# A three-layer kernel on one core: more yield points in the RWKV chain, a scan and two exponentials in halves, later transposes in stick-breaking attention

## The chip, the cores and the metric

The kernel runs on one core of a Trainium2 chip. The metric is the device time of one execution in microseconds (us), as the median of three runs. A core has TensorE (PE in the rows below), VectorE (DVE), ScalarE (ACT), GpSimd (POOL) and SyncE (SP), each with its own instruction stream that is worked off in order; they wait for each other through semaphores.

## What is computed

Three layers follow each other on 1024 tokens of width 1024, all in float32: a block with three mixing branches (stick-breaking attention, and two gated linear recurrences), a block with an RWKV-7 time mix and a dilated window attention, and a block with spatial gating and a Fourier mix. Two parts bear on the change. Stick-breaking attention, per head and per block of 128 queries:

```python
log_one_minus = jnp.where(causal, jax.nn.log_sigmoid(-z), 0.0)
tail = lax.cumsum(log_one_minus, axis=3, reverse=True) - log_one_minus
weights = masked_exp(causal, log_beta + tail)
outs.append(jnp.einsum('bhts,bhsd->bhtd', weights, vb.astype(jnp.float32)))
```

and the RWKV time mix, a recurrence over tokens for 16 heads of 64, followed by a group norm:

```python
def step(state, inp):
    r_t, w_t, k_t, v_t, av_t, bv_t = inp
    sa = jnp.einsum('bhvk,bhk->bhv', state, av_t)
    state = (state * w_t[:, :, None, :] + sa[..., None] * bv_t[:, :, None, :]
             + v_t[..., None] * k_t[:, :, None, :])
    return state, jnp.einsum('bhvk,bhk->bhv', state, r_t)
mu = jnp.mean(y, axis=-1, keepdims=True)
var = jnp.mean(jnp.square(y - mu), axis=-1, keepdims=True)
y = ((y - mu) * lax.rsqrt(var + GN_EPS)).reshape(B, S, RWKV_W) * ln_x_w + ln_x_b
```

## The kernel before, in words

**Dense products.** Large projections are split into a high and a low part and formed by three matmuls (L304 to L306). `dense_gen` makes such a product for 128 output columns and all tokens; it yields after every three matmuls. These rows are the bulk of TensorE's work and depend on little else; here they are called dense rows.

**How work is interleaved.** Each piece of work is a Python generator. `interleave` takes a list of generators, each with a number of steps and a range, and always advances the one whose position `a + (b - a) * steps done / steps given` is lowest. The order in which instructions are written is a priority: when the program is built, a scheduler puts the instructions of every engine into a fixed order, by that priority and by its own estimate of when operands are ready. A generator with more steps than it was given ends up behind the others, which are then exhausted.

**Stick-breaking (`stick`, twice, 8 query blocks each).** For a query block and two heads: score matmuls (L548), two sigmoids per score tile on ACT (L549, L550), on DVE a mask, a product scan over up to 1024 columns (L557) and a multiplication (L558); then 128x128 transposes on TensorE (L569), copies of these out of PSUM on DVE (L571), and the products with the values (L577). The generator is given 60 steps and has 60.

**RWKV (`rwkv`).** There are 16 units (8 head pairs by 2 halves of the tokens), in 18 iterations. In iteration `it` stand, interleaved: `rw_chain` of unit `it - 2`, `rw_inverse` of unit `it - 1`, `rw_feat` of unit `it`, and dense rows. Iterations 14 and 15 have fewer dense rows than the earlier ones, because the projections of head pair 8 do not exist.

`rw_chain` is a recurrence over 8 hops. One hop is: two products with the state (L1149) into PSUM; a copy of one half by DVE (L1150, tile R) and of the other by ACT (L1151, the scheduler lets it wait for DVE's); the product L1154; again a copy by DVE (L1155, tile SV) and by ACT (L1156); the products L1158 and L1163; and two DVE operations (L1162) that make the next state, on which the next hop's L1149 waits. There is one yield after each hop. Behind the last hop come the group norm (DVE, ACT, one power on POOL at L712), `GNY` = 4 yields, transposes (L1184) and a gate. The chain is given 11 + `GNY` = 15 steps.

`rw_feat` makes, among others, the decay: two products (L977, L978), two tanh on ACT, a scaling on POOL (L983), a scan of 512 columns on DVE (L985, a running sum within chunks of 64), two exponentials on ACT (L989, L990).

Of the kernel before, what the change touches and what calls it, by code (L numbers as in the profile page):

```python
# [12 lines left out]
AF = mybir.ActivationFunctionType  # L13
ALU = mybir.AluOpType
# [158 lines left out]
L3 = (0.2, 1.1)  # L173
WB = [(4,), (5, 3), (4,), (5,), (5,), (4, 3)]
MRB = 2
GNY = 4
V3 = (0.0, 0.8)
YD = 0
LNP = 4
# [15 lines left out]
PLAN = [(0.0, 1.0), (0.0, 0.5), (0.05, 0.8), (0.0, 1.0)]  # L195


class Kern:
# [328 lines left out]
    def stick(self, pm, pr, q, k, v, y):  # L527

        nc = self.nc
        for i in range(NT):  # L530
            W = 128 * (i + 1)
            bes = []
            qs = self.t(pm, [128, 2, 2, 128], "q2", F32R, bufs=1)
            for h in range(2):
                r = slice(64 * h, 64 * h + 64)
                src = q[r, 128 * i:128 * i + 128]
                for d in (r, slice(64 - 64 * h, 128 - 64 * h)):
                    nc.scalar.copy(qs[d, h, 0], src)
                for d in (slice(0, 64), slice(64, 128)):
                    nc.vector.tensor_tensor(qs[d, h, 1], src, qs[r, h, 0].bitcast(F32), ALU.subtract)  # L540
            for h in range(2):
                be = self.t(pm, [128, T], "be", bufs=3)
                om = self.t(pm, [128, T + 1], "om", bufs=2)
                for s0 in range(0, W, 512):
                    n = min(512, W - s0)
                    z = self.mm_ps()[:, :n]
                    for m in range(2):
                        nc.tensor.matmul(z, qs[:, h, m], k[h][:, s0:s0 + n], start=m == 0, stop=m == 1)  # L548
                    nc.scalar.activation(be[:, s0:s0 + n], z, AF.Sigmoid, scale=0.125)  # L549
                    nc.scalar.activation(om[:, s0:s0 + n], z, AF.Sigmoid, scale=-0.125)  # L550
                    yield
                dg = slice(W - 128, W)
                nc.vector.tensor_tensor(om[:, dg], om[:, dg], self.c("mge"), ALU.max)
                nc.vector.tensor_tensor(be[:, dg], be[:, dg], self.c("mlt"), ALU.mult)
                nc.gpsimd.memset(om[:, W:W + 1], 1.0)
                omr = om[:, W - 1::-1]
                nc.vector.tensor_tensor_scan(omr, omr, omr, 1.0, ALU.mult, ALU.min)  # L557
                nc.vector.tensor_tensor(be[:, :W], be[:, :W], om[:, 1:W + 1], ALU.mult)  # L558
                bes.append(be)
                yield  # L560
            po = self.mm_ps()[:, :128]
            for g0 in range(0, i + 1, 4):
                ws = []
                for b0 in range(g0, min(g0 + 4, i + 1), 2):
                    bl = [(h, b) for b in range(b0, min(b0 + 2, i + 1)) for h in range(2)]
                    wt = self.t(pm, [128, 4, 128], "wt", bufs=3)
                    pt = self.mm_ps()
                    for n, (h, b) in enumerate(bl):
                        nc.tensor.transpose(pt[:, 128 * n:128 * n + 128], bes[h][:, 128 * b:128 * b + 128], self.ident)  # L569
                    nb = len(bl)  # L570
                    nc.vector.tensor_copy(wt[:, :nb].rearrange("p a b -> p (a b)"), pt[:, :128 * nb])  # L571
                    ws.append((bl, wt))
                    yield
                for bl, wt in ws:
                    for n, (h, b) in enumerate(bl):
                        r = slice(64 * h, 64 * h + 64)
                        nc.tensor.matmul(po[r, :], v[:, b, 128 * pr + 64 * h:128 * pr + 64 * h + 64], wt[:, n], start=b == 0, stop=b == i)  # L577
            sl = slice(128 * i, 128 * i + 128)
            nc.vector.tensor_tensor(y[:, sl], po, y[:, sl], ALU.mult)
# [334 lines left out]
    def rwkv(self):  # L914
        nc, tc, I = self.nc, self.tc, self.I
        with tc.tile_pool(name="rw", bufs=1, reuse_waits="tile") as rw, self.psum(mx=2, iv=1, ch=1, cy=1):
            if RO:
                for n, shape, b in RORD:
                    self.t(rw, shape, n, bufs=b)
            self.consts(rw, "c2")  # L920
            self.XS = [self.t(rw, [128, 8, 128], f"XS{n}") for n in range(2)]
            self.SV = [self.t(rw, [128, 8, 2, 64], f"SV{n}") for n in range(2)]
            for x in self.XS:
                nc.gpsimd.memset(x, 0.0)
            for a in self.first:
                self.dense_fm(*a, hfs=(1,))
            for h in range(2):
                nc.scalar.activation(self.lov[h][0:64], self.lov[h][0:64], AF.Tanh)
            U = [dict(p=u // 2, hf=u % 2, u=u) for u in range(16)]
            self.jp = rw  # L930
            att = iter(self.att_jobs())
            for it in range(18):
                gens = []
                if it >= 2:
                    gens.append((self.rw_chain(rw, U[it - 2]), 11 + GNY, *PLAN[0]))
                if 1 <= it <= 16:
                    gens.append((self.rw_inverse(rw, U[it - 1]), 37, *PLAN[1]))
                if it < 16:
                    gens.append((self.rw_feat(rw, U[it]), 20, *PLAN[2]))
                jobs = list(islice(att, ATT[it]))  # L940
                gens.append((chain(*jobs, self.rw_dense(rw, it)), 32 * (it < 16) + 16 * len(jobs), *PLAN[3]))
                interleave(gens)
            self.late_jobs = list(att)
        self.rk_pool.__exit__(None, None, None)
# [18 lines left out]
    def rw_feat(self, rw, S):  # L963
        nc, I = self.nc, self.I
        V, TT = nc.vector, nc.vector.tensor_tensor
# [4 lines left out]
        c8 = lambda a: a.rearrange("p (c t) -> p c t", c=8)  # L970
        E, O = slice(0, 64), slice(64, 128)
        cc = float(np.exp(-0.5))
# [7 lines left out]
        sg, ta = ff("fs"), ff("ta")  # L980
# [1 line left out]
        nc.scalar.activation(ta, aps, AF.Tanh, bias=self.ha0[:, p:p + 1], scale=0.5)  # L982
        nc.gpsimd.tensor_scalar(sg, sg, 0.5, 0.5, ALU.mult, ALU.add)  # L983
        yield
        V.tensor_tensor_scan(sg, self.c("cm"), sg, 0.0, ALU.mult, ALU.add)  # L985
        e1 = self.t(rw, [128, 8, 65], "E1")
        ei = ff("ei")
        nc.gpsimd.memset(e1[:, :, 0:1], 1.0)
        nc.scalar.activation(e1[:, :, 1:65], c8(sg), AF.Exp, scale=-cc)  # L989
        nc.scalar.activation(ei, sg, AF.Exp, scale=cc)  # L990
        S["dc"] = dc = self.t(rw, [128, 8], "dc", bufs=3)
        nc.gpsimd.tensor_copy(dc, e1[:, :, 64])
        yield
# [46 lines left out]
        for c0 in (0, 4):  # L1040
            cs = slice(c0, c0 + 4)
# [84 lines left out]
    def rw_chain(self, rw, S):  # L1126
        nc = self.nc
        V, TT = nc.vector, nc.vector.tensor_tensor
# [7 lines left out]
        c8 = lambda a: a.rearrange("p (c t) -> p c t", c=8)  # L1136
# [6 lines left out]
        for c in range(8):  # L1143
            up, sp = [self.mm_ps("ch")[:, 0:w] for w in (64, 128)]
            sd = self.t(rw, [128, 64], "sd", bufs=2)
            R = self.t(rw, [128, 64], "R", bufs=2)
            dc = dcs[:, c:c + 1]
            for n, s in enumerate((E, O)):
                nc.tensor.matmul(xy[:, c, n], M1[:, c, n], sv[:, c, n], start=c % 4 == 0 and n == 0, stop=False, skip_group_check=True)  # L1149
            V.tensor_copy(R[E], xy[E, c, 0])  # L1150
            nc.scalar.copy(R[O], xy[O, c, 1])  # L1151
            for n, s in enumerate((E, O)):
                nc.scalar.activation(sd[s], sv[s, c, n], AF.Identity, scale=dc[s])  # L1153
            nc.tensor.matmul(up, xs[:, c], R, start=True, stop=True)  # L1154
            V.tensor_copy(sv[E, c, 0], up[E])  # L1155
            nc.scalar.copy(sv[O, c, 1], up[O])  # L1156
            both = sv[:, c].rearrange("p n v -> p (n v)")
            nc.tensor.matmul(sp, M3[:, c].rearrange("p n k -> p (n k)"), both, start=True, stop=True)  # L1158
            for n, s in enumerate((E, O)):
                if not (hf == 1 and c == 7):  # L1160
                    so = sv[s, c + 1, n] if c < 7 else svn[s, 0, n]
                    V.scalar_tensor_tensor(so, sp[s, 64 * n:64 * n + 64], dc[s], sd[s], ALU.mult, ALU.add)  # L1162
            nc.tensor.matmul(xy[:, c].rearrange("p n v -> p (n v)"), A[:, c], both, start=False, stop=c % 4 == 3, skip_group_check=True)  # L1163
            yield
# [6 lines left out]
        V.tensor_scalar(st[:, 0:8], st[:, 0:8], -1.0 / 64, None, ALU.mult)  # L1171
        TT(c8(y), c8(y), bc(st[:, 0:8]), ALU.add)
        nc.scalar.activation(sq, y, AF.Square)
        yield
        V.tensor_reduce(st[:, 8:16], c8(sq), AX.X, ALU.add)
        self.rsqrt(rw, st[:, 16:24], st[:, 8:16], 1.0 / 64, 64e-5)
        TT(c8(y), c8(y), bc(st[:, 16:24]), ALU.mult)
        for _ in range(GNY):
            yield
# [520 lines left out]
```

## Time and profile before

| | us |
|---|---|
| median of 3 runs | 2867.9 (2866.1 to 2868.88) |
| the profiled execution | 2864.67 |
| its span, first to last instruction | 2862.9 |
| PE busy | 2753.2 (96%) |
| DVE busy | 1754.1 (61%) |
| ACT busy | 1168.3 (41%) |
| POOL busy | 278.4 (10%) |

The profile shows one execution. Busy time of PE is a sum of modelled durations: a dense row is shown 0.39 us long while the next starts 0.23 us later, so a busy PE is not a PE at its peak. The stick-breaking part lies between about 60 and 330 us of the span, the RWKV part between about 920 and 2000 us; the chains run from 1070 us on.

### The profile page before, as it was taken

The page shows a single profiled execution, that of the slowest core. Times are in us where ns is not written, and L with a number is a line of the kernel's source. Part 1 is how long each engine was busy: PE and PEld are TensorE (multiplying, and loading weights), DVE is VectorE, ACT ScalarE, POOL GpSimd, SP SyncE. Part 2 cuts the span into 40 slices and gives each one's busy share as a digit, 9 for nine tenths or more (in the row PEclk, how much of TensorE's full clock was granted, in tenths as well). Part 3 has the DMA queues.
Part 4 walks back from the last instruction along what each step waited for, and adds up shares of the span by engine and source line. Part 5 has one row for each costly group of instructions (what it writes and reads, how often), then busy time and mean ns, then how long its engine had stood idle before and what let it go on. Part 6 is the DMA issues. An engine that isn't in the chain of part 4 may idle for free. (4 is left out here: it accounts for less than half of the span.)

```text
span 2862.9 us, 51271 instructions
## 1 busy us (share of the span) xinstructions
PE 2753.2 (96%) x19572; PEld 2303.7 (80%) x19572; DVE 1754.1 (61%) x4639; ACT 1168.3 (41%) x2830; POOL 278.4 (10%) x374
## 2 busy tenths in 40 slices
PE   9999999999999999999999999989999999999999
PEld 7778787777788787778877778768899989888869
DVE  4665533533867468786777877774476775633253
ACT  4443323223323325444455444534565665532222
POOL 0000000000222001100111111100111111101100
PEclk9999999999999999999999999989999999999999
DMA  3111111114753322222222222222764553421122
GB/s 123 51 60 49 53 67 35 60 57 164 228 181 107 94 80 68 71 75 74 72 71 74 75 61 75 83 56 81 217 188 144 159 163 100 142 100 52 41 96 75
DMA packets 212822, 273.70 MB, mean 96 GB/s; under 512 B 69840, under 2 KB 105184, under 8 KB 212448
## 3 DMA queue, kind: packets, MB, share of 16 engines
q1 hardware_dynamic: 184576, 217.98, 25.0%
q10 hardware_dynamic: 28000, 52.44, 5.0%
q8 instruction: 154, 2.52, 0.4%
q14 instruction: 92, 0.75, 0.1%
HBM read 210.57 MB, written 59.77 MB: 94 GB/s over the span
## 5 line engine op out<-in xcount | busy, mean ns | idle before, releaser
L304 PE MATMUL pd<-aH,wh 128*128 128x512 f32 (+1 forms) x1824 | 757.7, 415 | 13.0 <-ACT aH L299 6.1
L306 PE MATMUL pd<-aH,wl 128*128 128x512 f32 (+1 forms) x1824 | 735.3, 403 | 2.8 <-DVE wl L276 2.8
L305 PE MATMUL pd<-aL,wh 128*128 128x512 f32 (+1 forms) x1824 | 730.8, 401 | 0.0
L276 DVE TENSOR_TENSOR wl<-wraw,wh 128x512 fp32r<-128x512 f32 (+1 forms) x421 | 299.6, 718 | 318.2 <-ACT wh L275 306.5
L275 ACT CAST wh<-wraw 128x512 fp32r<-128x512 f32 (+1 forms) x421 | 255.3, 611 | 420.6 <-PE pd L305 236.1
L304 PEld LDWEIGHTS pd<-aH,wh 128*128 128x128 f32 (+1 forms) x1824 | 345.8, 190 | 85.1 <-issue 14.7
L306 PEld LDWEIGHTS pd<-aH,wl 128*128 128x128 f32 (+1 forms) x1824 | 345.0, 189 | 75.3 <-DVE wl L276 4.6
L305 PEld LDWEIGHTS pd<-aL,wh 128*128 128x128 f32 (+1 forms) x1824 | 346.2, 190 | 58.3 <-DVE aL L300 0.8
L304 PE MATMUL pd<-wh,aH 128*128 128x256 f32 x1088 | 319.2, 295 | 2.8 <-ACT wh L275 2.3
L305 PE MATMUL pd<-wl,aH 128*128 128x256 f32 x1088 | 309.9, 286 | 1.1 <-DVE wl L276 1.1
L306 PE MATMUL pd<-wh,aL 128*128 128x256 f32 x1088 | 307.7, 285 | 1.2 <-DVE aL L300 0.9
L304 PEld LDWEIGHTS pd<-wh,aH 128*128 128x128 f32 x1088 | 207.7, 191 | 7.9 <-ACT wh L275 3.2
L305 PEld LDWEIGHTS pd<-wl,aH 128*128 128x128 f32 x1088 | 208.3, 192 | 4.5 <-DVE wl L276 1.9
L306 PEld LDWEIGHTS pd<-wh,aL 128*128 128x128 f32 x1088 | 207.8, 191 | 2.3 <-DVE aL L300 2.0
L1427 ACT ACTIVATE S<-S,anm 128x256 f32<-128x256 f32 (+1 forms) x256 | 118.1, 462 | 21.0 <-DVE anm L1420 20.9
L1153 ACT ACTIVATE sd<-SV,dc 64x64 f32<-64x64 f32 x256 | 88.4, 345 | 83.6 <-DVE SV L1162 78.5
L1091 DVE TENSOR_TENSOR Xt<-At,X 128x60 f32<-128x60 f32 (+24 forms) x496 | 106.4, 214 | 11.1
L1093 DVE TENSOR_TENSOR X<-X,Xt 128x60 f32<-128x60 f32 (+24 forms) x496 | 104.8, 211 | 12.2
L1378 DVE CUSTOM_DVE_ANT_0 S<-sc,cf 128x256 f32<-128x256 f32 (+1 forms) x256 | 86.1, 377 | 32.3 <-PE sc L1375 21.4
L1374 PE MATMUL sc<-kk,qq 128*128 128x256 f32 (+1 forms) x256 | 90.4, 369 | 4.9 <-DVE kk L1349 3.3
L1149 PEld LDWEIGHTS cy<-SV,M 128*128 128x128 f32 x512 | 81.0, 193 | 16.3 <-DVE SV L1162 4.2
L1162 DVE SCALAR_TENSOR_TENSOR SV<-ch,dc,sd 64x64 f32<-64x64 f32 x240 | 67.9, 283 | 30.6 <-PE ch L1158 24.1
(348 smaller groups left out, 4894.7 us busy)
## 6 DMA issues: line engine op xcount, KB each, us to landing
wraw<-in_w2fm SPq DMA_DIRECT2D x122, 256.0 KB, 2.8
wraw<-in_w1fm SPq DMA_DIRECT2D x80, 256.0 KB, 2.6
qkr<-qkg SPq DMA_DIRECT2D x152, 128.0 KB, 2.9
wraw<-in_w2out SPq DMA_DIRECT2D x64, 256.0 KB, 3.4
sgd<-s ACTq DMA_DIRECT2D x48, 256.0 KB, 2.0
sgt<-sgd SPq DMA_DIRECT2D x48, 256.0 KB, 3.7
qkg<-ast ACTq DMA_DIRECT2D x42, 256.0 KB, 2.0
wraw<-in_w3fm SPq DMA_DIRECT2D x38, 256.0 KB, 2.6
```

Of the source, the lines that this page charges most:

```text
L275: nc.scalar.copy(h, raw)
L276: nc.vector.tensor_tensor(l, raw, h.bitcast(F32), ALU.subtract)
L304: mm(ps, lh, rh, start=start, stop=False)
L305: mm(ps, lh, rl, start=False, stop=False)
L306: mm(ps, ll, rh, start=False, stop=stop)
L1091: eng.tensor_tensor(tmp[:, :M, :n], At[:, j:j + 1, j + 1:32].to_broadcast([128, M, n]), X[:, :M, j:j + 1].to_broadcast([128, M, n]), ALU.mult)
L1093: eng.tensor_tensor(X[:, :M, j + 1:32], X[:, :M, j + 1:32], tmp[:, :M, :n], ALU.add)
L1149: nc.tensor.matmul(xy[:, c, n], M1[:, c, n], sv[:, c, n], start=c % 4 == 0 and n == 0, stop=False, skip_group_check=True)
L1153: nc.scalar.activation(sd[s], sv[s, c, n], AF.Identity, scale=dc[s])
L1374: mm(o, q, k, start=i == 0, stop=False, skip_group_check=True)
L1378: red = lambda o, x, mk, acc: V.tensor_tensor_reduce(o, x, mk, 1.0, -3e38, ALU.add, ALU.max, acc)
L1427: nc.scalar.activation(x, x, AF.Exp, bias=nm[:, n, h, t:t + 1], accum_out=l[:, n, h, t:t + 1])
```

## The change

Four edits, and step counts that go with them:

- `rw_chain` yields twice more in every hop: before L1154 and before L1158. It yields once more after the square of the group norm, and `GNY` is 8 instead of 4. It now has 36 steps and is given 38.
- `rw_feat`: the scan of 512 columns becomes two of 256 with a yield after each; the two exponentials become four of half the size, with a yield after each pair. It is given 22 steps instead of 20.
- `stick`: in query block `i` there are `1 + i // 3` yields between the weights and their transposes. It has 75 steps now; the number given (60) stays.

```diff
-GNY = 4
+GNY = 8
@@ stick
                 bes.append(be)
                 yield
+            for _ in range(1 + i // 3):
+                yield
             po = self.mm_ps()[:, :128]
@@ rwkv
-                    gens.append((self.rw_chain(rw, U[it - 2]), 11 + GNY, *PLAN[0]))
+                    gens.append((self.rw_chain(rw, U[it - 2]), 30 + GNY, *PLAN[0]))
...
-                    gens.append((self.rw_feat(rw, U[it]), 20, *PLAN[2]))
+                    gens.append((self.rw_feat(rw, U[it]), 22, *PLAN[2]))
@@ rw_feat
-        V.tensor_tensor_scan(sg, self.c("cm"), sg, 0.0, ALU.mult, ALU.add)
         e1 = self.t(rw, [128, 8, 65], "E1")
         ei = ff("ei")
         nc.gpsimd.memset(e1[:, :, 0:1], 1.0)
-        nc.scalar.activation(e1[:, :, 1:65], c8(sg), AF.Exp, scale=-cc)
-        nc.scalar.activation(ei, sg, AF.Exp, scale=cc)
+        halves = [(slice(256 * n, 256 * n + 256), slice(4 * n, 4 * n + 4)) for n in range(2)]
+        for tk, cs in halves:
+            V.tensor_tensor_scan(sg[:, tk], self.c("cm")[:, 0:256], sg[:, tk], 0.0, ALU.mult, ALU.add)
+            yield
+        for tk, cs in halves:
+            nc.scalar.activation(e1[:, cs, 1:65], c8(sg)[:, cs], AF.Exp, scale=-cc)
+            nc.scalar.activation(ei[:, tk], sg[:, tk], AF.Exp, scale=cc)
+            yield
@@ rw_chain
                 nc.scalar.activation(sd[s], sv[s, c, n], AF.Identity, scale=dc[s])
+            yield
             nc.tensor.matmul(up, xs[:, c], R, start=True, stop=True)
...
             both = sv[:, c].rearrange("p n v -> p (n v)")
+            yield
             nc.tensor.matmul(sp, M3[:, c].rearrange("p n k -> p (n k)"), both, start=True, stop=True)
...
         nc.scalar.activation(sq, y, AF.Square)
+        yield
         yield
```

Since a scheduler makes the order, the edits show best in what stands in a row on an engine. The line numbers of the changed kernel are shifted: L1149, L1150, L1154, L1155, L1158, L1162, L1163 are L1156, L1157, L1162, L1163, L1167, L1171, L1172 there; L977 and L978 are L979 and L980, L985 is L992, L1004 is L1011; L569 and L577 are L571 and L579.

DVE in the third unit, between hop 0 and hop 1 of its chain, before. `X` and `Xt` are tiles of the inverse, `fs` is the scan's, `R` and `SV` are the chain's copies, `kp` belongs to the features:

```order
L1093 TENSOR_TENSOR X_11914<-X_11914,Xt_11915 128x6x10
L1091 TENSOR_TENSOR Xt_11915<-At_11913,X_11914 128x6x9
L1093 TENSOR_TENSOR X_11914<-X_11914,Xt_11915 128x6x9
L985 SCALAR_TENSOR_TENSOR fs_11995<-cf_9411,fs_11995 128x512
L1150 COPY R_11974<-cy_11893 64x64
L1004 TENSOR_SCALAR kp_12088<-ta_11996,hka_9151,oka_9153 128x512
L1091 TENSOR_TENSOR Xt_11915<-At_11913,X_11914 128x6x8
L1005 TENSOR_TENSOR kp_12088<-kp_12088,rkv_1857_11126 128x512
L1155 COPY SV_1574_9415<-ch_11971 64x64
```

The same place on DVE after:

```order
L1100 TENSOR_TENSOR X_11919<-X_11919,Xt_11920 128x4x17
L1171 SCALAR_TENSOR_TENSOR SV_1574_9415<-ch_11907,dc_10798,sd_11908 64x64 x2
L992 SCALAR_TENSOR_TENSOR fs_12000<-cf_9411,fs_12000 128x256 x2
L1157 COPY R_11988<-cy_11905 64x64
L1098 TENSOR_TENSOR Xt_11920<-At_11918,X_11919 128x4x16
L1011 TENSOR_SCALAR kp_12153<-ta_12001,hka_9151,oka_9153 128x512
L1100 TENSOR_TENSOR X_11919<-X_11919,Xt_11920 128x4x16
L1012 TENSOR_TENSOR kp_12153<-kp_12153,rkv_1856_11125 128x512
L1163 COPY SV_1574_9415<-ch_11985 64x64
```

Both half scans still stand ahead of the copy R of hop 1, directly behind the state update of hop 0; in other units one row of the inverse stands between the halves.

TensorE at the same place, before (`pd` is a dense product's PSUM tile, `mx` takes the two feature products, `ch` and `cy` are the chain's):

```order
L304 MATMUL pd_11944<-aH_1096_7115,wh_11932 128x512
L305 MATMUL pd_11944<-aL_1097_7116,wh_11932 128x512
L1158 MATMUL ch_11895<-SV_1574_9415,M_1854_11094 128x128
L1163 MATMUL cy_11893<-SV_1574_9415,A_10854 128x128
L306 MATMUL pd_11944<-aH_1096_7115,wl_11933 128x512
L977 MATMUL mx_11962<-lo_9158,wa_11960 128x512
L978 MATMUL mx_11963<-lo_9158,wa_11960 128x512
L304 MATMUL pd_11944<-aH_1096_7115,wh_11932 128x512
L305 MATMUL pd_11944<-aL_1097_7116,wh_11932 128x512
L306 MATMUL pd_11944<-aH_1096_7115,wl_11933 128x512
L1149 MATMUL cy_11893<-SV_1574_9415,M_1817_10852 128x64 x2
```

and after:

```order
L304 MATMUL pd_11949<-aH_1096_7115,wh_11937 128x512
L305 MATMUL pd_11949<-aL_1097_7116,wh_11937 128x512
L306 MATMUL pd_11949<-aH_1096_7115,wl_11938 128x512
L979 MATMUL mx_11970<-lo_9158,wa_11968 128x512
L980 MATMUL mx_11971<-lo_9158,wa_11968 128x512
L1167 MATMUL ch_11907<-SV_1574_9415,M_1854_11118 128x128
L1172 MATMUL cy_11905<-SV_1574_9415,A_10914 128x128
L304 MATMUL pd_11949<-aH_1096_7115,wh_11937 128x512
L305 MATMUL pd_11949<-aL_1097_7116,wh_11937 128x512
L306 MATMUL pd_11949<-aH_1096_7115,wl_11938 128x512
L1156 MATMUL cy_11905<-SV_1574_9415,M_1828_10912 128x64 x2
```

The two feature products moved ahead of the end of hop 0. From hop 1's L1149 to its L1154 stand five dense rows before and six after; from hop 0's L1149 to its L1154 two before and six after.

TensorE where the last query block of the first stick-breaking pass begins, before (`q` marks the score products of that block, `wt` the copies of transposes of the block ahead):

```order
L577 MATMUL mx_1441<-wt_1476,tv_315 64x128 x4
L577 MATMUL mx_1441<-wt_1493,tv_315 64x128 x2
L548 MATMUL mx_1522<-f_44_191,q_250_1511 128x512 x2
L304 MATMUL pd_1489<-aH_5_70,wh_1414 128x512
L305 MATMUL pd_1489<-aL_6_71,wh_1414 128x512
L306 MATMUL pd_1489<-aH_5_70,wl_1415 128x512
L304 MATMUL pd_1489<-aH_5_70,wh_1420 128x512
L305 MATMUL pd_1489<-aL_6_71,wh_1420 128x512
L306 MATMUL pd_1489<-aH_5_70,wl_1421 128x512
L548 MATMUL mx_1533<-f_44_191,q_250_1511 128x512 x2
```

and after:

```order
L571 MATMUL mx_1586<-cf_157,be_1429 128x128
L571 MATMUL mx_1586<-cf_157,be_1464 128x128
L548 MATMUL mx_1608<-f_44_191,q_261_1597 128x512 x2
L548 MATMUL mx_1613<-f_44_191,q_261_1597 128x512
L579 MATMUL mx_1540<-wt_1578,tv_315 64x128 x4
L579 MATMUL mx_1540<-wt_1585,tv_315 64x128 x2
L548 MATMUL mx_1613<-f_44_191,q_261_1597 128x512
L548 MATMUL mx_1625<-f_45_192,q_261_1597 128x512 x2
L548 MATMUL mx_1630<-f_45_192,q_261_1597 128x512 x2
L304 MATMUL pd_1703<-aH_3_68,wh_1691 128x512
L305 MATMUL pd_1703<-aL_4_69,wh_1691 128x512
```

There the pass has run out of its dense rows, and the score products of the last block stand in a row. Behind them come 14 dense rows of the next pass, one transpose pair, 12 more dense rows, and the rest of the transposes. The second pass ends in the same way. In most of the earlier query blocks the last score products are followed by 12 to 15 dense rows before the first transpose in the kernel before, and by 18 to 30 after. Outside stick-breaking and RWKV the order of the instructions is the same in both kernels.

## Rows read from the trace of the kernel before

**Rows 1.** The page's busy time of TensorE: us, share, instructions
```profile
PE 2753.2 (96%) x19572; PEld 2303.7 (80%) x19572; DVE 1754.1 (61%) x4639; ACT 1168.3 (41%) x2830; POOL 278.4 (10%) x374
```

**Rows 2.** Waits of PE, 60 to 330 us: who for whom, us, times, longest
```profile
PE mx L569 <- DVE be L558: 10.7, 11, 1.3
PE mx L577 <- DVE wt L571: 1.0, 1, 1.0
```

**Rows 3.** Waits of PE, 1060 to 1990 us, same columns
```profile
PE ch L1154 <- ACT R L1151: 17.6, 18, 1.7
PE ch L1184 <- DVE tt L1177: 7.8, 6, 2.6
PE ch L1158 <- ACT SV L1156: 2.3, 6, 0.6
```

**Rows 4.** Timeline of TensorE, hops 0 and 1 of the third unit: start us, us, instruction
```profile
1199.84 0.43 PE L1154 MATMUL ch<-R,XS 128*128 128x64 f32 x2 [0.19 <-ACT R L1151]
...
1202.47 0.69 PE L977 MATMUL mx<-lo,wa 64*128 64x512 f32 x1
...
1204.33 0.55 PE L1149 MATMUL cy<-SV,M 128*128 128x64 f32 x4
...
1205.47 0.39 PE L304 MATMUL pd<-aH,wh 128*128 128x512 f32 x1
1205.70 0.40 PE L305 MATMUL pd<-aL,wh 128*128 128x512 f32 x1
1207.55 0.43 PE L1154 MATMUL ch<-R,XS 128*128 128x64 f32 x2 [1.46 <-ACT R L1151]
```

**Rows 5.** Timelines of POOL, DVE and ACT around the same hop 1
```profile
1204.54 0.62 POOL L983 TENSOR_SCALAR fs<-fs 128x512 f32<-128x512 f32 x1 [1.82 <-ACT fs L981]
...
1205.38 1.22 DVE L985 TENSOR_TENSOR_SCAN fs<-cf,fs 128x512 f32<-128x512 f32 x1
1206.63 0.22 DVE L1150 COPY R<-cy 64x64 f32<-64x64 f32 x1
...
1208.02 0.22 DVE L1155 COPY SV<-ch 64x64 f32<-64x64 f32 x1
...
1206.64 0.63 ACT L989 ACTIVATE E<-fs 128x512 f32<-128x512 f32 x1 [1.68 <-DVE fs L985]
1207.29 0.21 ACT L1151 COPY R<-cy 64x64 f32<-64x64 f32 x1
```

**Rows 6.** Timeline of PE: hop 1 of the first and of the thirteenth unit
```profile
1082.39 0.43 PE L1154 MATMUL ch<-R,XS 128*128 128x64 f32 x2 [1.70 <-ACT R L1151]
...
1810.98 0.43 PE L1154 MATMUL ch<-R,XS 128*128 128x64 f32 x2 [1.49 <-ACT R L1151]
```

**Rows 7.** The stick-breaking scan: ns min/median/max, first and last start, forms
```profile
L557 DVE TENSOR_TENSOR_SCAN om<-om x32: 409/1352/2291, 36.2 to 311.5; 128x128 f32<-128x128 f32 x4, 128x256 f32<-128x256 f32 x4, 128x384 f32<-128x384 f32 x4, 128x512 f32<-128x512 f32 x4
```

**Rows 8.** Timelines of PE and DVE, last query block of the second pass
```profile
302.96 0.73 PE L548 MATMUL mx<-f,q 128*128 128x512 f32 x2
...
311.17 0.41 PE L569 MATMUL mx<-cf,be 128*128 128x128 f32 x2 [1.02 <-DVE be L558]
...
309.81 1.22 DVE L558 TENSOR_TENSOR be<-be,om 128x1024 f32<-128x1024 f32 x1
```

**Rows 9.** Timelines of DVE and PE at a group norm's end
```profile
1670.83 0.69 DVE L1177 TENSOR_TENSOR tt<-tt,gst 128x512 f32<-128x512 f32 x1 [2.13 <-POOL gst L712]
...
1671.57 0.66 PE L1184 MATMUL ch<-cf,tt 128*128 128x128 f32 x4 [1.20 <-DVE tt L1177]
```

**Rows 10.** Stretches: us, busy (instructions) of PE, PEld, DVE, ACT, POOL; PE clock, DMA, GB/s
```profile
1063.00:1120.00 57.00, 55.22 (x355) 44.06 (x354) 48.05 (x142) 25.48 (x64) 6.41 (x11) 1.00 0.22 60
...
1880.00:1890.00 10.00, 6.12 (x27) 4.64 (x27) 8.15 (x35) 4.06 (x12) 0.00 (x0) 0.69 0.00 1
1890.00:1900.00 10.00, 7.77 (x43) 6.62 (x43) 8.50 (x17) 2.01 (x4) 0.66 (x1) 0.80 0.21 33
1900.00:1910.00 10.00, 5.26 (x75) 4.38 (x76) 3.76 (x7) 3.98 (x10) 2.02 (x3) 0.54 0.26 76
```

## Prediction, made before the changed kernel ran

> **What bounds the kernel now.** I began with the page's busy times: TensorE is busy for 96% of the span [rows 1]. So only what makes TensorE stand still can be won, and the next view is who TensorE waited for, in the two parts that the change touches. In stick-breaking it waits 10.7 us in eleven waits for the weights of a query block and once for 1.0 us [rows 2]. In the RWKV part it waits 17.6 us in 18 waits for ACT's copy R, 7.8 us for the end of group norms, and 2.3 us for SV [rows 3]. That is 39.4 us in 48 waits with the whole cost of each a little larger: dense rows start 0.23 us apart, but are drawn 0.40 long. In hop 1 of the third unit the last dense row starts at 1205.70, the next could start at 1205.93, and L1154 starts at 1207.55 [rows 4]. It lost 1.62 us where the profile shows 1.46, so 0.16 is added per wait. All of it gone would be 39.4 + 48 x 0.16, or 47 us: the ceiling, short of waits too small to be shown.
>
> The third view is the timeline of a long wait. The 18 waits for R hold ten of 1.26 to 1.70 us and one of 0.75, all in hop 1 of a unit, the first and the last long one in [rows 6]. Hop 1's L1149 starts at 1204.33 [rows 4], but DVE has the feature scan of 1.22 us ahead of the copy R, and that scan itself had to wait for POOL's scaling, which ran from 1204.54 to 1205.16. R is copied at 1206.63, ACT then puts an exponential of 0.63 us ahead of its own half, at 1207.29 [rows 5], and L1154 follows 0.26 later.
>
> **Stick-breaking.** The extra yields put 6 to 15 more dense rows between scores and transposes in most blocks, 1.4 to 3.5 us at 0.23, against waits of at most 1.3 [rows 2]. They cover them all: 11.7 us plus 12 x 0.16, so 13.6 won. But 15 of now 75 steps come after the pass has used up its dense rows, twice. From the first score product to the first transpose the last block took 311.17 - 302.96 = 8.2 us [rows 8]; six dense rows stood there between the first two score products (1.4 us), so the dependency needs some 6.8. After the change 8 score products and 14 dense rows stand there, 22 x 0.23 = 5.1, with a few short products some 5.6: 1.2 lost. The second head then needs 2.29 [rows 7] + 1.22 [rows 8] of DVE and two masks, about 4 us, against 12 dense rows (2.8): 1 lost. Transposes and products without dense rows between them, 0.8. So 3 us per tail, 6 in all; the bounds are 3 and 10. Net -8 (-11 to -3).
>
> **Hop 1 of the chain.** Time is counted from the feature product L977 (1202.47). Before: POOL starts at 2.07, the scan runs from 2.91 to 4.13, L1154 starts at 5.08, and TensorE was ready at 3.46 [rows 4, 5]. After, the order puts L977 ahead of hop 0's last two products and one more dense row ahead of L1154. TensorE is then ready about 0.4 (estimate for four short passes) + 0.23 later, at 4.1. A scan takes 409 ns for 128 columns and 2291 for 1024 [rows 7], that is 0.14 us plus 2.1 ns a column: 0.68 for a half, 1.36 for both. They still stand together ahead of R, so R comes no earlier: 4.3, or 4.5 where an inverse row stands between. What shrinks is ACT: the first pair of half exponentials (0.32 to 0.63 each, from half to the whole [rows 5]) can run while the second half scan does. ACT's copy starts at 4.5 to 4.8, L1154 at 4.8 to 5.1. Lost: about 0.8 instead of 1.62; for eleven units -9. The next copy, SV, waits on DVE behind feature rows, as it did from 1206.85 to 1208.02 [rows 5]; one inverse row more stands there, and only three dense rows instead of five ahead of L1158. I give back 0.35 in 13 units, +4. Net -5, from -13 (nothing given back, all covered) to +3.
>
> [...]
>
> **Hop 0.** It loses 0.19 + 0.16 at L1154 in the unit shown [rows 4]; the order now has six dense rows there instead of two, which covers it, and L1158 stands behind the two feature products. I take 0.36 in 13 of the units: -5 (-8 to 0, since most of these losses are too small for the profile to show).
>
> **Other hops.** Their yields move a dense row here and there; 2.3 us of waits for SV and some 2 us for R [rows 3] are there to be won, but dense rows are also taken from the gap ahead of L1149. -2 (-8 to +5).
>
> **Group norm.** TensorE waits for it six times, 7.8 us [rows 3]; the wait shown ends with POOL's power and a DVE multiplication [rows 9]. With four yields more, the order keeps about 10 us of TensorE work between the last hop and L1184 in most units, while in the later units the DVE rows queued ahead of the norm become fewer. Two of the six stand in the last units without dense rows and stay. -4 (-9 to +3).
>
> **Last units.** [...] The changed order leaves about half a hop more uncovered: +2 (-4 to +9).
>
> **Added work.** 16 scans of 0.14 us extra on DVE and 32 exponentials on ACT. DVE is busy 48 of 57 us in an early unit [rows 10] and has 9 us left for an added 0.14. Nothing, at most +2.
>
> **Sum.** -8 - 5 - 5 - 2 - 4 + 2 = -22. The profiled execution took 2864.67 us, so 2842.7; the median of 2867.9 is 3.2 higher, so **2846**.
>
> **Rivals.** (1) *The waits move.* Hop 1's gain returns at L1158 and at the next L1149, hop 0's gain was never there, the stick tails take the upper bound of 10: -3 in all, 2865. For it: the half scans still stand together ahead of R. Against it: the stick waits are plain and their cover is doubled. (2) *The group norm becomes each unit's bound* and it is slower. The chain ends later, so fewer TensorE rows lie behind its last hop, and the norm's own steps give way to others on a DVE that is busy 48 of 57 us [rows 10]; L1184 then stops TensorE in all 16 units. At 2.4 us each, near the longest wait [rows 3], that is +38; with the other terms at -18 it comes to +20, 2888. It turns slower from 18 / 16 = 1.1 us per unit on. Against it: DVE has fewer rows queued there than before. (3) *Everything is covered*: all 47 us less about 1, 2822. Against it: the tails, and the scans ahead of R. (4) *The stretch of the last units doubles* [rows 10]: another 10.8 us idle, and about 6 us of slow clock (0.32 of the clock missing over some 19 busy us). +17 there in place of +2, so -7: 2861. [...]
>
> **Chances.** The forecast (2833 to 2859) 0.60, rival 1 0.13, rival 2 0.10, rival 3 0.12, rival 4 0.05. The terms' bounds, which will not all fall on one side, give the forecast about 13 us to either side; with rival 1 and half of rival 3 the range is 2826 to 2866. Differences of 0.2%, 5.7 us, can be told from no change. Faster: 0.60 + 0.12 + most of rival 4, 0.76; the same: rival 1 and the rest of rival 4, 0.14; slower: rival 2, 0.10.
>
> **What would show it.** In stick-breaking the waits at the first transposes should be gone but for the two tails, at 1 to 2 us each. In hop 1 of a unit the wait for R should be about 0.65 instead of 1.46, and a wait for SV should stand behind it. Waits for the group norm should be below 5 us in all. Wrong would be: waits for R still above 1.2 us in hop 1, tails above 5 us each, L1184 waiting in most units, or a longer stretch without dense rows around 1880 us.

## The result and the profile after

The changed kernel took 2843.14 us (median of four runs, 2840.7 to 2849.28) beside 2867.0 for the kernel before: a ratio of 0.992, 95% interval 0.9902 to 0.9938, so 24 us faster. The prediction was 2846 (2826 to 2866). The execution profiled after took 2849.28 us, the longest of its four, so the two profiles differ by only 15.4 us. TensorE's busy time answers to [rows 1]; its share stays at 96% of a shorter span:

```profile
PE 2745.1 (96%) x19572; PEld 2305.1 (81%) x19572; DVE 1742.6 (61%) x4655; ACT 1172.3 (41%) x2862; POOL 277.3 (10%) x374
```

To see in which stage the time went, take one line's last start in each (count, ns min/median/max, first and last start, forms). For the kernel before these are the last products of linear attention, the group norm's transposes and attention's score products:

```profile
L734 PE MATMUL mx<-cf,o x32: 272/273/303, 363.5 to 682.0; 128*128 128x128 f32 x32
L1184 PE MATMUL ch<-cf,tt x64: 270/272/474, 1125.2 to 2004.3; 128*128 128x128 f32 x64
L1374 PE MATMUL sc<-kk,qq x256: 218/365/605, 2022.3 to 2390.6; 128*128 128x256 f32 x80, 128*128 128x128 f32 x48
```

The same lines of the changed kernel:

```profile
L736 PE MATMUL mx<-cf,o x32: 272/273/303, 360.2 to 677.9; 128*128 128x128 f32 x32
L1194 PE MATMUL ch<-cf,tt x64: 270/272/474, 1121.0 to 1985.9; 128*128 128x128 f32 x64
L1384 PE MATMUL sc<-kk,qq x256: 218/365/605, 2003.4 to 2375.5; 128*128 128x256 f32 x80, 128*128 128x128 f32 x48
```

Stick-breaking and its partner are done 4.1 us earlier, the RWKV part 18.4 (so 14.3 of its own), attention 15.1: it gave back 3.3 in a part that the change doesn't touch. One profile is not exact to the microsecond. In a second one of the changed kernel (run `changed_again`, 2844.82 us) the first stage alone ended 10.3 us early; of the other two, the RWKV part took 12.5 us less than before and attention 2.0 more:

```profile
L736 PE MATMUL mx<-cf,o x32: 272/273/302, 355.6 to 671.7; 128*128 128x128 f32 x32
L1194 PE MATMUL ch<-cf,tt x64: 270/272/476, 1114.5 to 1981.5; 128*128 128x128 f32 x64
L1384 PE MATMUL sc<-kk,qq x256: 218/372/603, 1999.2 to 2369.8; 128*128 128x256 f32 x80, 128*128 128x128 f32 x48
```

The waits in stick-breaking, against [rows 2] (who for whom, us, times, longest), and the four of them that make the two tails, one tail around 185 us, one around 314:

```profile
PE mx L571 <- DVE be L558: 4.6, 5, 1.1
```
```profile
183.58 0.41 PE L571 MATMUL mx<-cf,be 128*128 128x128 f32 x2 [1.13 <-DVE be L558]
187.75 0.84 PE L571 MATMUL mx<-cf,be 128*128 128x128 f32 x6 [1.00 <-DVE be L558]
...
311.53 0.41 PE L571 MATMUL mx<-cf,be 128*128 128x128 f32 x2 [1.13 <-DVE be L558]
316.23 0.87 PE L571 MATMUL mx<-cf,be 128*128 128x128 f32 x6 [0.62 <-DVE be L558]
```

The waits outside the tails are gone but for one of 0.8 us at 295. In the RWKV part (1060 to 1990 us, against [rows 3]) the wait for R fell from 17.6 to 6.8 and that for the norm from 7.8 to 3.4, but the second row is new: L1156, the first product of a hop, waits for the state that L1171 writes. It had 0.2 us before.

```profile
PE ch L1162 <- ACT R L1158: 6.8, 15, 1.1
PE cy L1156 <- DVE SV L1171: 5.6, 10, 0.7
PE ch L1167 <- ACT SV L1164: 3.9, 7, 0.6
PE ch L1194 <- DVE tt L1187: 3.4, 3, 1.6
```

Hops 0 and 1 of the third unit, against [rows 4]:

```profile
1193.95 0.33 PE L1162 MATMUL ch<-R,XS 128*128 128x64 f32 x2
...
1195.50 0.59 PE L979 MATMUL mx<-lo,wa 64*128 64x512 f32 x1
...
1196.02 0.49 PE L1167 MATMUL ch<-SV,M 128*128 128x128 f32 x2
...
1197.90 0.76 PE L1156 MATMUL cy<-SV,M 128*128 128x64 f32 x4 [0.47 <-DVE SV L1171]
...
1200.01 0.43 PE L1162 MATMUL ch<-R,XS 128*128 128x64 f32 x2
...
1201.75 0.49 PE L1167 MATMUL ch<-SV,M 128*128 128x128 f32 x2 [0.55 <-ACT SV L1164]
```

Hop 0 no longer waits at L1162. The feature products (L979) now stand ahead of hop 0's last products, as the order had said. Hop 1 has no wait for R left here, but one ahead of it, for the state, and one behind it, for SV.

The last units, against [rows 10] (us, busy of PE, PEld, DVE, ACT, POOL; clock, DMA, GB/s): the stretch without dense rows has moved 20 us forward and is as long as before, 18.25 busy of 30 us in place of 19.15, at much the same granted clock (a mean of 0.66 in place of 0.68).

```profile
1860.00:1870.00 10.00, 5.93 (x22) 4.47 (x22) 7.53 (x35) 3.09 (x11) 0.00 (x0) 0.63 0.01 2
1870.00:1880.00 10.00, 8.07 (x46) 7.48 (x46) 7.05 (x12) 1.79 (x4) 0.00 (x0) 0.69 0.20 31
1880.00:1890.00 10.00, 4.25 (x74) 3.01 (x74) 4.29 (x9) 6.28 (x16) 2.67 (x3) 0.65 0.23 61
```

### The profile page after: what moved, and what is told of

Read it like the earlier page. It is cut to its first block, busy times and chain, and to the rows that moved or that the text cites. A ratio compares the mean times of both kernels' runs of the same rounds, so it can differ in the third digit from the quotient of the medians.

```text
span 2847.5 us, 51317 instructions
## 1 busy us (share of the span) xinstructions
PE 2745.1 (96%) x19572; PEld 2305.1 (81%) x19572; DVE 1742.6 (61%) x4655; ACT 1172.3 (41%) x2862; POOL 277.3 (10%) x374
## 4 chain that ended last, share of the span: by engine, by line
PE 44%; DVE 6%; issue 3%; ACT 2%; DMA 2%; POOL 1%; ACTq 0%; DVEq 0%; SPq 0%; POOLq 0%
PE pd L304 8%; PE pd L305 8%; PE pd L306 8%; PE po L1462 2%; PE mx L1053 2%; PE tr L1472 1%; PE sc L1384 1%; PE sc L1385 1%; PE cy L1156 1%; PE mx L305 1%; PE mx L304 1%; PE mx L306 1%; DVE wl L276 1%; PE ch L1167 1%; DVE X L1100 1%
## 5 line engine op out<-in xcount | busy, mean ns | idle before, releaser
L306 PE MATMUL pd<-aH,wl 128*128 128x512 f32 (+1 forms) x1824 | 727.7, 399 | 3.5 <-DVE wl L276 3.5
L1437 ACT ACTIVATE S<-S,anm 128x256 f32<-128x256 f32 (+1 forms) x256 | 118.0, 463 | 19.6 <-DVE anm L1430 19.6
L1100 DVE TENSOR_TENSOR X<-X,Xt 128x60 f32<-128x60 f32 (+24 forms) x496 | 105.6, 213 | 11.1
L1098 DVE TENSOR_TENSOR Xt<-At,X 128x60 f32<-128x60 f32 (+24 forms) x496 | 106.3, 214 | 9.9
L1156 PEld LDWEIGHTS cy<-SV,M 128*128 128x128 f32 x512 | 80.4, 192 | 29.1 <-DVE SV L1171 17.6
L1384 PE MATMUL sc<-kk,qq 128*128 128x256 f32 (+1 forms) x256 | 90.8, 370 | 7.0 <-DVE kk L1359 6.1
L1156 PE MATMUL cy<-SV,M 128*128 128x64 f32 x512 | 83.9, 271 | 6.2 <-DVE SV L1171 5.6
```

The lines of the kernel that those rows point to most:

```text
L306: mm(ps, ll, rh, start=False, stop=stop)
L1098: eng.tensor_tensor(tmp[:, :M, :n], At[:, j:j + 1, j + 1:32].to_broadcast([128, M, n]), X[:, :M, j:j + 1].to_broadcast([128, M, n]), ALU.mult)
L1100: eng.tensor_tensor(X[:, :M, j + 1:32], X[:, :M, j + 1:32], tmp[:, :M, :n], ALU.add)
L1384: mm(o, q, k, start=i == 0, stop=False, skip_group_check=True)
L1437: nc.scalar.activation(x, x, AF.Exp, bias=nm[:, n, h, t:t + 1], accum_out=l[:, n, h, t:t + 1])
```

## The experiments

All ratios are to the kernel before, run beside them on the same chip. Line numbers are each kernel's own.

| run | what it is | median us | ratio, 95% interval |
|---|---|---|---|
| only_stick | before + stick-breaking yields | 2860.5 | 0.9967 (0.9957, 0.9977) |
| only_chain | before + chain yields | 2895.7 | 1.0097 (1.0080, 1.0114) |
| only_halves | before + halves | 2870.1 | 1.0004 (0.9993, 1.0014) |
| only_norm | before + norm yields | 2878.5 | 1.0025 (1.0012, 1.0038) |
| no_halves | changed, halves undone | 2854.9 | 0.9945 (0.9933, 0.9958) |
| no_norm | changed, norm yields undone | 2874.7 | 1.0022 (1.0013, 1.0032) |
| act_scale | changed, scaling on ACT | 2841.2 | 0.9905 (0.9892, 0.9918) |
| count75 | changed, stick count 75 | 2846.6 | 0.9924 (0.9911, 0.9937) |
| changed_again | the changed kernel | 2844.3 | 0.9922 (0.9910, 0.9935) |
| best | act_scale and count75 | 2837.6 | 0.9898 (0.9883, 0.9912) |
| norm12 | changed, 12 norm yields | 2850.0 | 0.9943 (0.9930, 0.9957) |
| pool_twice | changed, second scaling | 2849.7 | 0.9943 (0.9930, 0.9955) |

### Each part of the change alone

**only_stick**

```diff
                 bes.append(be)
                 yield
+            for _ in range(1 + i // 3):
+                yield
             po = self.mm_ps()[:, :128]
```

> The kernel before with nothing but the added yields in stick-breaking. The prediction's term for them is -8 us (-11 to -3): 13.6 won at the first transposes, some 6 given back in two tails. In the trace of the changed kernel the point at which this stage and its linear-attention partner are through comes 5 us earlier, so I now expect -5, about 0.998 of the time before. The rival, in which the tails take everything back, says 0, and the rival in which all waits are covered says -12.

It gained 9.5 us (12.3 to 6.6): the prediction's -8 holds, the tails don't take everything back, and the rival with all waits covered, -12, stands at the interval's end. The -5 read off the trace of the changed kernel was too little.

**only_chain**

```diff
-                    gens.append((self.rw_chain(rw, U[it - 2]), 11 + GNY, *PLAN[0]))
+                    gens.append((self.rw_chain(rw, U[it - 2]), 30 + GNY, *PLAN[0]))
...
+            yield
             nc.tensor.matmul(up, xs[:, c], R, start=True, stop=True)
...
+            yield
             nc.tensor.matmul(sp, M3[:, c].rearrange("p n k -> p (n k)"), both, start=True, stop=True)
```

> The kernel before with only the two added yields in each hop of the chain and the count of 30 in place of 11; the scan and the exponentials stay whole and the norm keeps its yields. By the prediction hop 0 gives -5, other hops -2, the last units +2, and of hop 1's -5 the part that comes from a later product, about -7 + 4 = -3: together -8. If instead hop 1's gain is only moved to the next wait, for the state, as the trace of the changed kernel suggests, it is -5. If the yields alone carry the RWKV part's whole gain in that trace, it is -15.

Every expectation was wrong, and by far: it is 28 us slower. The waits say why (1060 to 2020 us):

```profile
PE ch L1155 <- ACT R L1151: 19.6, 17, 2.3
PE ch L1186 <- DVE tt L1179: 18.6, 10, 3.0
PE ch L1186 <- DVE Xt L1091: 7.0, 5, 2.0
```

TensorE waits at the group norm's transposes (L1186) 15 times, 25.6 us, where it had six waits of 7.8 [rows 3]. The wait for R is no shorter than before (19.6 against 17.6). The interleaving gives each step of a generator the same share of the unit. The chain counted 15 steps, four of them the norm's; now it counts 34, still with four, so the norm has 4/34 of a unit instead of 4/15 to be worked out in; no_norm below tests this.

**only_halves**

```diff
-        V.tensor_tensor_scan(sg, self.c("cm"), sg, 0.0, ALU.mult, ALU.add)
+        for tk, cs in halves:
+            V.tensor_tensor_scan(sg[:, tk], self.c("cm")[:, 0:256], sg[:, tk], 0.0, ALU.mult, ALU.add)
+            yield
...
+        for tk, cs in halves:
+            nc.scalar.activation(e1[:, cs, 1:65], c8(sg)[:, cs], AF.Exp, scale=-cc)
+            nc.scalar.activation(ei[:, tk], sg[:, tk], AF.Exp, scale=cc)
+            yield
```

> The kernel before with only the feature scan and its exponentials in halves and three more steps of that generator (count 22). By the prediction ACT's copy of R comes some 0.3 us sooner in hop 1 of about eleven units, -3 us, and nothing else changes. The rival holds the halves alone for the cause of the shorter wait for R (from 1.5 to about 0.5 us): -10. A second rival has the added steps take cover from other hops: +3.

No difference in time: the expected -3 lies just outside the interval, the second rival's +3 inside it. The nothing is a net of several shifts. R is waited for 15.8 us in place of 17.6 and the norm 1.8 in place of 7.8, but two later lines of the features, L1051 and L1060, wait for DVE for 9.6 us, where they had 0.8. So the added scans and exponentials have no net cost that can be told; what they cost by themselves isn't isolated.

**only_norm**

```diff
-GNY = 4
+GNY = 8
...
         nc.scalar.activation(sq, y, AF.Square)
         yield
+        yield
```

> The kernel before with only the group norm's added yields (8 for 4, and one more ahead of the second reduction). By the prediction -4 us (-9 to +3), and waits for the normalised tile at the transposes of under 4 us in place of 7.8. The rival: those waits went through the chain's yields, which shift the norm too, and the norm's own yields alone bring 0, or a few us more, since the chain without its other yields then ends each unit late.

The waits for the norm are nearly gone (1.7 us), and yet it is 7 us slower: the rival, with a few us more, was right. By the same rule the eight hops now share a smaller part of the unit, with fewer dense rows between two hops. R is waited for 28 times instead of 18, but for less in all, 13.7 us in place of 17.6. What grew are the waits of the inverse's products, from 0.3 us to 9.1, and of the features' L1046 for the tile At, from nothing to 4.3 (1060 to 2020 us). That the smaller share of the hops is what makes these wait was not tested:

```profile
PE ch L1154 <- ACT R L1151: 13.7, 28, 1.2
PE iv L1112 <- DVE Xt L1109: 9.1, 9, 1.4
PE mx L1046 <- DVE At L1036: 4.3, 3, 3.8
...
PE ch L1185 <- DVE tt L1178: 1.7, 2, 1.3
```

The four parts alone add up to -9.5 + 28 + 0 + 7, some 26 us slower. Together they are 24 faster. So the parts depend on one another, and the next runs took one away from the whole.

### One part taken away, one cause changed

**no_halves**: the changed kernel with the `-` and `+` lines of only_halves undone.

> The changed kernel with the whole scan and whole exponentials again (count 20); stick-breaking, chain and norm as changed. The halves alone measured 0, so if the parts only add, this takes the time of the changed kernel. If the halves are what makes the added yields of the chain pay in hop 1, as the prediction has it for ACT's shorter lead, it is slower by 3 to 9 us, and the waits for R in hop 1 are again above 1.2 us.

Slower by some 7 us than the changed kernel's 0.992. R and the norm (L1189) are waited for longer, 9.6 and 7.0 in place of 6.8 and 3.4. So halves that were worth nothing alone are worth something once the chain's yields are there. The time is as the second expectation said; of its waits, two in hop 1 are above 1.2 us (1.32 and 1.31, where the changed kernel has 1.09), and the others there are 0.6 or less.

```profile
PE ch L1157 <- ACT R L1153: 9.6, 16, 1.3
PE ch L1189 <- DVE tt L1182: 7.0, 7, 3.0
```

**no_norm**: the changed kernel with the edit of only_norm undone.

> The changed kernel with the norm's old yields (4, one fewer ahead of the second reduction). The theory after the first four runs: the chain's count went from 15 to 34, so four yields of the norm are 4/34 of a unit instead of 4/15, and TensorE reaches the norm's transposes before the norm is done in most units; that cost 28 us when the chain's yields stood alone, and should cost as much here: some 2870 to 2875, with waits at the norm's transposes of about 25 us. The prediction's own term for the norm's yields, 4 us, says 2847 with waits of some 8 us.

As the theory of the shares said: 2874.7, with 24.6 us of waits for the norm in thirteen units. The norm's yields are worth 29 us in this kernel, where they cost 7 alone. The wait for R is back too, 18.1 us where the changed kernel has 6.8, while that for the state is down to 0.5. The feature products stand ahead of hop 0's last products here as well, but in the third unit six dense rows instead of three stand ahead of hop 1's L1156, and three instead of six between it and L1162. So the two waits trade places with where the dense rows fall.

```profile
PE ch L1193 <- DVE tt L1186: 24.6, 13, 5.3
PE ch L1162 <- ACT R L1158: 18.1, 19, 1.9
```

**act_scale**

```diff
         nc.scalar.activation(sg, wps, AF.Tanh, bias=self.hw0[:, p:p + 1], scale=0.5)
+        nc.scalar.activation(sg, sg, AF.Copy, bias=0.5, scale=0.5)
         nc.scalar.activation(ta, aps, AF.Tanh, bias=self.ha0[:, p:p + 1], scale=0.5)
-        nc.gpsimd.tensor_scalar(sg, sg, 0.5, 0.5, ALU.mult, ALU.add)
```

> The changed kernel with the feature scaling by 0.5 and 0.5 on ACT between the two tanhs instead of on POOL. In the trace of the changed kernel a VectorE operation that begins beside POOL's scaling ends only when that ends (0.5 to 0.7 us for one of 0.22), and in hop 1 the state update behind it is late, for which TensorE waits at the product of the masked matrix with the state (5.6 us in ten waits, some 10 us by starts). If that stall makes the new wait, it shrinks and the time falls by 4 to 8 us. If the state update is late because of its place in VectorE's queue, nothing changes (0 to +3, for 0.6 us more of ACT per unit).

The wait for the state fell from 5.6 to 1.7 us and that for R from 6.8 to 4.8; the one for SV behind them rose from 3.9 to 6.7. By the ratios the time is some 4 us below the changed kernel's, less than the intervals can separate.

```profile
PE ch L1167 <- ACT SV L1164: 6.7, 15, 0.6
...
PE cy L1156 <- DVE SV L1171: 1.7, 6, 0.4
```

**count75**

```diff
-M1 = [60, 60, 46, 46, 78]
+M1 = [75, 75, 46, 46, 78]
```

> The changed kernel with the count of the two stick-breaking passes at 75, the steps that they now have, instead of 60, so that dense rows last to the end of each pass. The prediction gave 3 us to each of the two tails; in the trace of the changed kernel five waits of 0.6 to 1.1 us stand there, 4.6 us, or 5.4 with 0.16 for each. If that is the tails' whole price and the fewer rows per step still cover the rest, the time falls by 4 to 5 us. The rival: with a fifth fewer dense rows per step the waits come back in the other blocks, and it is the same or slower by up to 5.

The tails' waits are gone (one of 0.2 left), but two others of 1.1 and 1.0 us came elsewhere, and the time can't be told from the changed kernel's. The tails are real, and what they cost is below what these runs resolve.

```profile
PE mx L571 <- ACT om L550: 1.1, 1, 1.1
PE mx L579 <- DVE wt L573: 1.0, 1, 1.0
PE mx L571 <- DVE be L558: 0.2, 1, 0.2
```

### The dose, the cause and a better kernel

**changed_again**: no edit.

> The changed kernel once more, beside the three below on one chip, so that they can be held against it directly. Expected: 2843 within 3 us, a ratio of 0.992.

As expected.

**norm12**

```diff
-GNY = 8
+GNY = 12
```

> The changed kernel with 12 yields of the norm in place of 8 (the count goes with it, 42). The theory: the norm's yields buy time between the last hop and the transposes, and pay with the hops, which are pressed into a smaller share of the unit. Four yields gave 2875, eight 2843; at eight only three waits for the norm, 3.4 us, are left, so there is little to win and more waits in the hops and the inverse: slower by 3 to 10 us, as the norm's yields alone were. The rival, that more room for the norm is better still, says -3.

Slower by 5.6 us: four (no_norm, which has one yield fewer besides), eight and twelve give 2875, 2844 and 2850. TensorE hardly waits less for the norm (2.8 for 3.4), and for R twice as long. The wait of L1156 for the state (L1171), 5.4 us in changed_again, is not there any more; in the third unit the feature products stand behind hop 0's last products again, as in the kernel before. So the hops' waits traded places here too, and the rise for R is not what the hops lost in all:

```profile
PE ch L1162 <- ACT R L1158: 14.2, 15, 1.4
...
PE ch L1194 <- DVE tt L1187: 2.8, 3, 1.9
```

**pool_twice**

```diff
         nc.gpsimd.tensor_scalar(sg, sg, 0.5, 0.5, ALU.mult, ALU.add)
+        nc.gpsimd.tensor_scalar(sg, sg, 1.0, 0.0, ALU.mult, ALU.add)
```

> The changed kernel with a second scaling on POOL, by 1 and 0, behind the first, so that POOL's work beside hop 0's end is doubled. If POOL's operation holds up whatever VectorE has begun beside it, a VectorE operation stands beside each of the two, the state update of hop 0 is later by up to 0.6 us, and the wait for the state in hop 1 grows from 5.6 to 9 us or more in all. If nothing is held up, VectorE's rows beside the second stay at 0.2 us, the wait for the state stays, and only R is later, since the scan starts 0.65 later. Both have the time rise, by 3 to 9 us; the rows tell them apart.

Slower by 5.4 us. The wait for the state grew to 9.1 us, that for R stayed (6.4):

```profile
PE cy L1157 <- DVE SV L1172: 9.1, 11, 1.2
PE ch L1163 <- ACT R L1159: 6.4, 11, 1.2
```

The same place of one unit in three kernels shows how the scaling delays the state. The changed kernel, timelines of POOL, DVE and PE:

```profile
1553.36 0.62 POOL L985 TENSOR_SCALAR fs<-fs 128x512 f32<-128x512 f32 x1 [11.23 <-DVE X L1100]
...
1553.37 0.66 DVE L1098 TENSOR_TENSOR Xt<-At,X 128x48 f32<-128x48 f32 x1
...
1554.19 0.59 DVE L1171 SCALAR_TENSOR_TENSOR SV<-ch,dc,sd 64x64 f32<-64x64 f32 x2
...
1554.51 0.76 PE L1156 MATMUL cy<-SV,M 128*128 128x64 f32 x4 [0.69 <-DVE SV L1171]
```

With the second scaling:

```profile
1551.11 0.62 POOL L985 TENSOR_SCALAR fs<-fs 128x512 f32<-128x512 f32 x1 [11.23 <-ACT fs L983]
1551.81 0.62 POOL L986 TENSOR_SCALAR fs<-fs 128x512 f32<-128x512 f32 x1
...
1551.18 0.60 DVE L1099 TENSOR_TENSOR Xt<-At,X 128x48 f32<-128x48 f32 x1
1551.82 0.67 DVE L1101 TENSOR_TENSOR X<-X,Xt 128x48 f32<-128x48 f32 x1
...
1552.73 0.76 PE L1157 MATMUL cy<-SV,M 128*128 128x64 f32 x4 [1.14 <-DVE SV L1172]
```

With the scaling on ACT, DVE and PE:

```profile
1550.54 0.21 DVE L1098 TENSOR_TENSOR Xt<-At,X 128x48 f32<-128x48 f32 x1
...
1551.23 0.76 PE L1156 MATMUL cy<-SV,M 128*128 128x64 f32 x4 [0.24 <-DVE SV L1171]
```

The inverse's row takes 0.21 us by itself and 0.66 beside POOL's scaling: it ends when that ends. Two scalings hold up two rows. The state update stands behind them in VectorE's queue, and in this unit TensorE's wait goes 0.24, 0.69, 1.14, a step of 0.45 for each scaling.

**best**: the edits of act_scale and count75 together.

> The changed kernel with the feature scaling on ACT and the stick-breaking count of 75 together. Alone they came to 0.9905 and 0.9924 beside the changed kernel's 0.992, neither told apart from it. Their traces show the waits that each was to take away gone (the first transposes 4.6 to about 1 us, the state's 5.6 to 1.7), so together I expect -5 us against the changed kernel, some 2838; the rival, that the waits only move on (to SV, which rose from 3.9 to 6.7), says 0.

2837.6 us, 6.7 below changed_again beside it, with intervals that touch (0.9912 and 0.9910); all its runs (2829.65 to 2840.0) lie below all of changed_again's (2840.51 to 2844.82). It is faster than the kernel before by 28 us; that it beats the changed kernel is likely, on four runs and five.

## Why the prediction was right, and where its steps were not

The total was right to 3 us, in part by luck: the parts were not all right, and their errors cancelled. To count what a wait list hides, I took for each TensorE product how much later it starts after its predecessor than the same pair of shapes usually does (the 20th percentile), and summed that by line and hop over the 16 units ("lost by starts").

- **Stick-breaking, -8.** Measured alone -9.5. The waits went as said; the tails were put at 6 us and show 3.9 us of waits, and doing away with them won nothing that can be told.
- **Hop 1, -5.** This step failed. The wait for R fell by more than was said (lost by starts, 19.1 to 7.0 us; predicted -9). But the give-back was put at 4 us, and it was 13: L1149, now L1156, went from 2.3 to 12.8, and L1158, now L1167, from 2.6 to 5.4. Hop 1 as a whole lost 24.0 us before and 25.2 after. The prediction had read from the order that the feature products move ahead of hop 0's last two products, and had not followed what comes with them: POOL's scaling then falls on VectorE's rows just ahead of hop 0's state update (0.66 us for a row of 0.21 in the unit shown above). That is a part of the rise only: with the scaling on ACT (act_scale) the same count at L1156 is 8.1, so 4.7 of the 10.5 us went with it. What the rest hangs on is argued from the order alone: in no_norm, with three dense rows more ahead of L1156, and in norm12, with the feature products behind hop 0 in most units, the wait for the state is all but gone and R waits instead. Nor is the shorter wait for R the work of the halves alone: undoing them brings back 2.8 of the 10.8 us, and undoing the norm's yields, which the prediction did not connect with hop 1, all of it (18.1). Rival 1 had named the next L1149 as the place, so that part of it came true. Hop 0's last two products, whose 0.4 us was an estimate, take 0.47 in the third unit (L1167 at 1196.02, the next dense row at 1196.49).
- **Hop 0, -5.** Right where it was looked for: lost by starts at L1154 and L1158 in the first fourteen units, 6.8 us before and 1.9 after. The fifteenth unit's hop 0 gave 3.5 back there in new waits; with the hop's other line the sums are 11.3 and 8.4.
- **Other hops, -2.** 35.6 before, 36.6 after: nothing, within the bounds given.
- **Group norm, -4.** Its waits fell by 4.4 us (lost by starts 10.0 to 4.5). The number was right, but the price of the chain's yields was missing beside it: without the norm's own yields they would have cost 29 us. Rival 2, at 0.10, described this very mechanism, at 38 us; what keeps it away is the norm's own yields, which the prediction put into this term without saying what the kernel would be without them.
- **Last units, +2.** Idle 11.8 us of 30 in place of 10.9: +1. The half hop more behind the +2 was my estimate from the order, and no run shows it: the stretch without dense rows is as long as before.
- **Added work, 0.** The halves alone measured 1.0004, the net of shorter and longer waits.
- **Not foreseen.** In the RWKV part the hops together won only 0.7 us by starts (70.9 before, 70.2 after); the norm won 5.5. The rest of that part's gain lies in small gaps: dense rows some -4 (TensorE changes from other products to dense rows some 330 times instead of some 370 from the third to the thirteenth unit) and the inverse's L1112 and L1118 -3.3. No run isolates these, so their cause stays open, as does the 3.3 us that attention lost in the profile; its first wait for keys (L1384) was 6.1 us there and 4.0 in the second profile, 3.3 before.

So the RWKV part's -14 was met (14.3, and 12.5 in the second profile), but from other terms than those it was made of.

Two sums of the prediction are off, without changing the forecast. The ceiling counts 48 waits where its rows hold 42, so it is 46 us and not 47. Rival 1's -3 is the stick term alone at its upper bound (13.6 less 10); with the prediction's own terms for the other hops, the norm and the last units it would be about -8, or 2860.

## What to carry to other kernels

Where generators share a timeline by step counts, a yield in one place takes a share of the unit from every other place of that generator: adding yields to the hops starved the norm and cost 28 us, and adding yields to the norm alone cost 7, with longer waits in other generators; only both together paid. Test the parts of such a change together and by leaving one out, since none of them alone showed what it was worth. When a wait for one copy is cured, follow the same queue to the operation behind it: here the wait moved from R to the state, and hop 1 as a whole won nothing.

## What the runs showed of the hardware

In the trace of the changed kernel, a row of the inverse (L1098, L1100) that begins beside POOL's scaling does not end before it. One does so in 14 of the 16 units: it takes 0.50 to 0.68 us, where the median of all these rows is 0.21, and ends 0.04 to 0.08 us after the scaling. In pool_twice two scalings hold two rows (0.60 and 0.67). I had counted POOL's 0.62 us as time on another engine.

The kernel before had it too, beside the scaling of 1204.54 to 1205.16 [rows 5], but there the scan, which waits for the scaling anyway, stood behind the row that was held:

```profile
1204.56 0.66 DVE L1091 TENSOR_TENSOR Xt<-At,X 128x54 f32<-128x54 f32 x1
```

The state update is not held itself where a scaling runs beside it: in pool_twice a pair of them that starts at 1193.02 and runs on beside the second scaling (1193.11 to 1193.73) takes 0.59 us, as long as the pair at 1554.19 in the changed kernel, which has no scaling beside it. Why the one kind of row is held and the other is not, no run shows.
